# First projection of the last SwiGLU mixer: 19 of 22 tile pairs by seven half-size products

## The chip, the cores and the metric

The kernel runs on one core of a Trainium2 chip. The metric is the device time of one execution in microseconds. A core has a matrix engine (PE, whose weight loads are listed as PEld), a vector engine (DVE), an activation engine (ACT), a general engine (POOL), and a queue engine (SP) that issues most transfers. They run side by side, each through its own instructions in order, and wait for each other by semaphores. Matmuls write to PSUM, eight banks of 128 x 512 float32 numbers.

## The reference, cut to what matters

A decoder trunk over 512 tokens of width 1024: a Mamba layer, a dense SwiGLU mixer, an attention layer, and a second SwiGLU mixer, which ends the kernel. The change is in the second mixer's first projection.

```python
def swiglu(h, w_in, w_out):
    a, b = jnp.split(h @ w_in, 2, axis=-1)
    return (jax.nn.silu(a) * b) @ w_out
...
    h = adaln(x, norm_pre_ffn[i], sh_f, sc_f)
    x = x + g_f[:, None, :] * rmsnorm(swiglu(h, ffn_w_in[i], ffn_w_out[i]), norm_post_ffn[i])
```

Here h is 512 x 1024, w_in 1024 x 5632 (a and b are 2816 columns each, 22 tiles of 128), w_out 2816 x 1024, all float32.

## The kernel before, in words

Every float32 factor x is split into two fp32r parts (`split`, lines 112 and 113): hi, a rounded copy that ACT makes, and lo = x - hi, which DVE makes. A product is then three matmuls (`mm3`, lines 133 to 135): hi by hi, hi by lo, lo by hi. A matmul has 128 x 128 weights and up to 512 moving columns.

The activations h stand transposed: 8 tiles (k) of 128 features by 512 tokens, each a pair (hi, lo). Weights come from memory in units of 128 x 1024, which are 8 blocks of 128 x 128 (512 KB). `split_unit` loads a unit into a `raw` buffer (4 of them) through SP and splits it into a `w` buffer (3 pairs).

In the mixer (`ffn`, i = 1), `win` walks over the tile pairs f = 0 to 21; a pair is one tile of a and one of b, so two units. The first three pairs go through `linear_start`: the six units are split into held `b` tiles, and all six banks are filled for the first 256 tokens and then for the other 256, since the second half of h is finished later. Each of the other 19 pairs is two calls of `linear` into the two `acc` banks: 8 k by 3 matmuls of 512 columns each. Then ACT takes Silu of a (L425), DVE multiplies by b (L426) and the result is split into `mid` (L112, L113). After the last pair `project_out` makes the second projection (L276 to L278) with `mid` as its weights, first for output columns 0 to 511 into four `seg` banks (22 k by 4 by 3 matmuls), then for the other 512.

The second half of h comes from the attention layer's output: x is written (L346), its rows are scaled (`unit_rows`, with the small `rsqrt` steps L186 to L199 on DVE), turned by PE transposes (L240), scaled and shifted (L248, L250) and split.

The order of instructions on each engine is laid down when the program is built, by a planner: program order is the priority, an instruction is placed when its inputs and buffers are due by the planner's own estimates, and so an engine can be given later work ahead of earlier work that would wait. On the chip that order is fixed. Tiles of a pool with n buffers make the n+1st wait for the release of the first. The pools that matter are `rawp` (raw), `wp` (w), `t2` (8 small work tiles, named t), `b4` (33 tiles of 4 KB a partition, named b), and PSUM with 2 acc, 4 seg and 2 mi banks.

Of the kernel before, what the change touches and what calls it, by code (L numbers as in the profile page):

```python
# [9 lines left out]
F32 = mybir.dt.float32  # L10
F32R = mybir.dt.float32r
BF16 = mybir.dt.bfloat16
I32 = mybir.dt.int32
AF = mybir.ActivationFunctionType
OP = mybir.AluOpType
AX = mybir.AxisListType

P = 128
# [3 lines left out]
KD = D // P  # L22
KF = DFF // P
# [9 lines left out]
HALVES = [slice(0, S // 2), slice(S // 2, S)]  # L33
# [7 lines left out]
class Weights:  # L41


    def __init__(self, kern, dram, start=0):
        self.kern, self.dram = kern, dram
        self.unit, self.skip, self.left = start // 8, start % 8, 0
        self.queue = []
# [21 lines left out]
        return [(hi[:, i * P:(i + 1) * P], lo[:, i * P:(i + 1) * P]) for i in range(8)]  # L69


class Kernel:
    def __init__(self, ctx, tc, a):
        self.tc, self.nc, self.a = tc, tc.nc, a
        pool = lambda name, bufs=1, **kw: ctx.enter_context(tc.tile_pool(name=name, bufs=bufs, **kw))
        self.const = pool("const")
        self.rawp = pool("rawp", 4)
        self.wp = pool("wp", 3)
        self.t2 = pool("t2", 8)
        self.b4 = pool("b4", 33)  # L80
        self.small = pool("small", 2)
        self.psum = pool("psum", 3, space=bass.MemoryType.PSUM)
        self.dram = pool("dram", 1, space=bass.MemoryType.DRAM)
# [35 lines left out]
    def split_unit(self, dram, held=False):  # L119
        nc = self.nc  # L120
        raw = self.rawp.tile([P, 1024], F32, name="raw")
        nc.sync.dma_start(raw, dram)
        if held:
            hi, lo = self.big((P, 1024), F32R), self.big((P, 1024), F32R)
        else:
            w = self.wp.tile([P, 2, 1024], F32R, name="w")
            hi, lo = w[:, 0], w[:, 1]
        self.split(hi, lo, raw)
        return hi, lo

    def mm3(self, ps, wh, wl, xh, xl, start, stop):
        nc = self.nc
        nc.tensor.matmul(ps, wh, xh, start=start, stop=False)  # L133
        nc.tensor.matmul(ps, wh, xl, start=False, stop=False)  # L134
        nc.tensor.matmul(ps, wl, xh, start=False, stop=stop)  # L135

    def linear(self, weights, x, ps=None):

        ps = self.acc() if ps is None else ps
        for k, (xh, xl) in enumerate(x):  # L140
            wh, wl = weights.next()
            self.mm3(ps, wh, wl, xh, xl, k == 0, k == len(x) - 1)
        return ps

    def linear_start(self, weights, x, count, parts):

# [268 lines left out]
    def ffn(self, i, h, x_src, x_dst):  # L415
        nc = self.nc
        win = Weights(self, self.a[f"ffn_in{i}"])
        mods = [] if i else list(range(40, 112))
        start, each = MODS_FFN
        mid = []  # L420
        pss = self.linear_start(win, h, 6, HALVES)
        for f in range(KF):
            pa, pb = pss[2 * f:2 * f + 2] if f < 3 else (self.linear(win, h), self.linear(win, h))
            s = self.tmp()
            nc.scalar.activation(s, pa, AF.Silu)  # L425
            nc.vector.tensor_tensor(out=s, in0=s, in1=pb, op=OP.mult)  # L426
            m = self.big(dt=F32R)
            self.split(m[:, 0], m[:, 1], s)
            mid.append((m[:, 0], m[:, 1]))
            if f >= start:  # L430
                for j in mods[(f - start) * each:(f - start + 1) * each]:
                    self.mod(j, j in MODS_BEHIND)
        gain = self.scale_cols(("post_ffn", 8 * i), 48 * i + 40, 0.0)
        first = [self.seg() for _ in range(4)]
        if i:
            return self.project_out(self.a["ffn_out1"], mid, x_src, gain, x_dst, first)
        keep = [self.big() for _ in range(KD // 2)]
        keep = [keep[k // 2][:, k % 2] for k in range(KD)]
        h, after = self.before(("kv_norm", 0), 96, keep)
        self.project_out(self.a["ffn_out0"], mid, x_src, gain, x_dst, first, after)  # L440
        return h, keep


    def conv(self, ps, j):
# [628 lines left out]
CST_M, _ = _places([("tri", 128), ("mask_t", 128)])  # L1073
CST_A, _ = _places([("mask_q", 128), ("add_pe", 128), ("cmp_add", 128), ("cmp_ok", 128)])
# [25 lines left out]
def _blocks(w, order):  # L1100

    k, n = w.shape
    b = w.reshape(k // P, P, n // P, P).transpose(0, 2, 1, 3)
    i = np.array(order)
    b = b[i[:, 0], i[:, 1]]
    return np.ascontiguousarray(b.reshape(-1, 8, P, P).transpose(0, 2, 1, 3)).reshape(-1, P, 8 * P)


def _plain(w, tiles=None):
    k, n = w.shape[0] // P, w.shape[1] // P  # L1110
    return _blocks(w, [(i, j) for j in (range(n) if tiles is None else tiles) for i in range(k)])
# [14 lines left out]
def prepare(i):  # L1126
    g = {k: np.asarray(v) for k, v in i.items()}
# [19 lines left out]
                          + [(k, n) for n in tiles[6:] for k in range(KD)])  # L1147
    r["ssm_out"] = _halves(g["ssm_w_out"][0])
    for j in range(2):
        tiles = [t for f in range(KF) for t in (f, KF + f)]  # L1150
        r[f"ffn_in{j}"] = _plain(g["ffn_w_in"][j], tiles)
        r[f"ffn_out{j}"] = _halves(g["ffn_w_out"][j])
    w = g["w_kv"]
    k = _plain(w, [0, 1, 2, 3, 4, 5, 8, 9])
# [25 lines left out]
```

## Time and profile before

| | us |
|---|---|
| median of 3 runs (1556.65 to 1556.98) | 1556.92 |
| profiled execution, its own time | 1556.36 |
| its span from first to last instruction | 1554.3 |
| PE busy | 1485.1 |
| DVE busy | 997.8 |
| ACT busy | 710.3 |
| POOL busy | 83.2 |

Times on the timeline count from the first instruction. In a row of the timeline stand the start, the duration, the engine, the line, the operation, what it writes and reads, the shape and the count, and in brackets the idle time before it and what ended it. A matmul's duration contains the drain of the array, so the distance from one start to the next is its cost in a stream. Consecutive DVE operations overlap by some 0.08 us in the same way.

### The profile page before, as it was taken

The page shows a single profiled execution, that of the slowest core. Times are in us where ns is not written, and L with a number is a line of the kernel's source. Part 1 is how long each engine was busy: PE and PEld are TensorE (multiplying, and loading weights), DVE is VectorE, ACT ScalarE, POOL GpSimd, SP SyncE. Part 2 cuts the span into 40 slices and gives each one's busy share as a digit, 9 for nine tenths or more (in the row PEclk, how much of TensorE's full clock was granted, in tenths as well). Part 3 has the DMA queues.
Part 4 walks back from the last instruction along what each step waited for, and adds up shares of the span by engine and source line. Part 5 has one row for each costly group of instructions (what it writes and reads, how often), then busy time and mean ns, then how long its engine had stood idle before and what let it go on. Part 6 is the DMA issues. An engine that isn't in the chain of part 4 may idle for free.

```text
span 1554.3 us, 20592 instructions
## 1 busy us (share of the span) xinstructions
PE 1485.1 (96%) x7806; PEld 1204.2 (77%) x7806; DVE 997.8 (64%) x1798; ACT 710.3 (46%) x1216; POOL 83.2 (5%) x91
## 2 busy tenths in 40 slices
PE   6999899999999999999999999999999999999998
PEld 4767676767889787888889877777678888888886
DVE  7876776788594887862366778878857233333246
ACT  3574839384463223232366565555646222222233
POOL 0040303040000000000000100000000000000000
PEclk9999999999999999999999999999999999999999
DMA  8443253455672888863565452312244122232254
GB/s 297 160 137 101 63 166 92 149 176 204 233 249 70 304 297 288 287 241 102 182 205 204 113 170 62 82 42 69 55 163 149 41 95 98 99 103 95 95 203 149
DMA packets 71956, 236.62 MB, mean 152 GB/s; under 512 B 8465, under 2 KB 12049, under 8 KB 71858
## 3 DMA queue, kind: packets, MB, share of 16 engines
q1 hardware_dynamic: 71570, 235.07, 45.8%
q8 instruction: 61, 1.00, 0.3%
q10 hardware_dynamic: 288, 0.25, 0.1%
q14 instruction: 37, 0.30, 0.1%
HBM read 215.30 MB, written 8.45 MB: 144 GB/s over the span
## 4 chain that ended last, share of the span: by engine, by line
PE 66%; DVE 13%; DMA 10%; issue 5%; ACT 4%; POOL 1%; SPq 1%; DVEq 0%; ACTq 0%; POOLq 0%
PE acc L133 10%; PE acc L134 10%; PE acc L135 10%; PE seg L277 5%; PE seg L278 5%; PE seg L276 5%; DMA raw<-in_mod_dram 3%; PE acc L277 3%; PE acc L278 3%; PE acc L276 3%; DVE w L113 2%; DVE raw L160 2%; DMA raw<-in_ffn_in_dram 2%; PE mi L1030 2%; DMA b<-b 2%
## 5 line engine op out<-in xcount | busy, mean ns | idle before, releaser
L113 DVE TENSOR_TENSOR w<-raw,w 128x1024 fp32r<-128x1024 f32 x233 | 289.1, 1242 | 259.9 <-ACT w L112 259.3
L112 ACT ACTIVATE w<-raw 128x1024 fp32r<-128x1024 f32 x233 | 245.8, 1057 | 373.0 <-PE seg L278 121.2
L133 PE MATMUL acc<-b,w 128*128 128x512 f32 x976 | 388.8, 399 | 12.5 <-ACT w L112 4.9
L134 PE MATMUL acc<-b,w 128*128 128x512 f32 x976 | 385.1, 395 | 0.8 <-DVE b L113 0.8
L135 PE MATMUL acc<-b,w 128*128 128x512 f32 x976 | 385.1, 395 | 0.1
L133 PEld LDWEIGHTS acc<-b,w 128*128 128x128 f32 x976 | 184.6, 190 | 55.7 <-ACT w L112 6.1
L135 PEld LDWEIGHTS acc<-b,w 128*128 128x128 f32 x976 | 184.9, 189 | 40.6 <-issue 1.6
L134 PEld LDWEIGHTS acc<-b,w 128*128 128x128 f32 x976 | 185.3, 190 | 39.5 <-DVE b L113 1.9
L160 DVE SCALAR_TENSOR_TENSOR raw<-raw,b 128x1024 f32<-128x1024 f32 x112 | 137.5, 1235 | 26.9 <-DMA raw<-in_mod_dram 25.8
L276 PE MATMUL seg<-w,b 128*128 128x512 f32 x340 | 132.7, 391 | 0.0
L278 PE MATMUL seg<-w,b 128*128 128x512 f32 x340 | 132.6, 390 | 0.0
L277 PE MATMUL seg<-w,b 128*128 128x512 f32 x340 | 132.3, 389 | 0.0
L999 ACT ACTIVATE b<-seg,nm 128x512 f32<-128x512 f32 (+3 forms) x128 | 66.0, 525 | 51.8 <-DVE nm L994 49.3
L112 ACT ACTIVATE b<-t 128x512 fp32r<-128x512 f32 (+1 forms) x108 | 55.1, 529 | 49.2 <-DVE t L426 39.5
L278 PEld LDWEIGHTS seg<-w,b 128*128 128x128 f32 x340 | 63.8, 188 | 13.3
L277 PEld LDWEIGHTS seg<-w,b 128*128 128x128 f32 x340 | 63.8, 188 | 13.1
L276 PEld LDWEIGHTS seg<-w,b 128*128 128x128 f32 x340 | 63.9, 188 | 13.0
L426 DVE TENSOR_TENSOR t<-t,acc 128x512 f32<-128x512 f32 x40 | 27.4, 685 | 63.0 <-PE acc L135 63.0
L425 ACT ACTIVATE t<-acc 128x512 f32<-128x512 f32 x40 | 23.7, 593 | 94.5 <-PE acc L135 94.4
L276 PE MATMUL acc<-w,b 128*128 128x512 f32 x164 | 64.0, 392 | 1.6 <-ACT w L112 1.6
L277 PE MATMUL acc<-w,b 128*128 128x512 f32 x164 | 64.1, 391 | 1.3 <-DVE w L113 1.3
L113 DVE TENSOR_TENSOR b<-t,b 128x512 fp32r<-128x512 f32 (+1 forms) x108 | 59.1, 567 | 8.4 <-ACT b L112 8.2
(287 smaller groups left out, 2396.0 us busy)
## 6 DMA issues: line engine op xcount, KB each, us to landing
raw<-in_mod_dram SPq DMA_DIRECT2D x112, 512.0 KB, 4.6
raw<-in_ffn_in_dram SPq DMA_DIRECT2D x88, 512.0 KB, 4.4
raw<-in_ffn_out_dram SPq DMA_DIRECT2D x66, 512.0 KB, 3.7
raw<-in_ssm_in_dram SPq DMA_DIRECT2D x41, 512.0 KB, 4.3
raw<-in_ssm_out_dram SPq DMA_DIRECT2D x24, 512.0 KB, 4.4
b<-acsd SPq DMA_DIRECT2D x40, 256.0 KB, 5.8
b<-b SPq DMA_DIRECT2D x32, 256.0 KB, 4.7
raw<-in_kv_dram SPq DMA_DIRECT2D x12, 512.0 KB, 4.4
```

The lines of the kernel that those rows point to most:

```text
L112: nc.scalar.activation(hi, src, AF.Copy)
L113: nc.vector.tensor_tensor(out=lo, in0=src, in1=hi.bitcast(F32), op=OP.subtract)
L133: nc.tensor.matmul(ps, wh, xh, start=start, stop=False)
L134: nc.tensor.matmul(ps, wh, xl, start=False, stop=False)
L135: nc.tensor.matmul(ps, wl, xh, start=False, stop=stop)
L160: i = nc.vector.scalar_tensor_tensor(out=raw, in0=raw, scalar=1.0, in1=self.cs, op0=OP.mult, op1=OP.mult, accum_out=self.modc[:, n:n + 1])
L276: nc.tensor.matmul(ps, x[0][:, ts], wh, start=start, stop=False)
L277: nc.tensor.matmul(ps, x[0][:, ts], wl, start=False, stop=False)
L278: nc.tensor.matmul(ps, x[1][:, ts], wh, start=False, stop=stop)
L426: nc.vector.tensor_tensor(out=s, in0=s, in1=pb, op=OP.mult)
L999: nc.scalar.activation(p[i], bank[:, at:at + n], AF.Exp, bias=nm[:, i:i + 1], accum_out=d[:, i:i + 1])
L1030: nc.tensor.transpose(ps[:, i * n + a * P:i * n + (a + 1) * P], unit["p"][j * per + i][:, a * P:(a + 1) * P], self.ident)
```

## The change

For the 19 pairs f = 3 to 21 of the last mixer, the product of h (2 halves of tokens by 2 halves of k) with the pair's weights (2 halves of k by the two tiles a and b) is made as a 2 x 2 block product by seven products of half size instead of eight (the Winograd form of Strassen's method). With A for h and B for the weights, the left sums are s1 = a21 + a22, s2 = s1 - a11, s3 = a11 - a21, s4 = a12 - s2, and the right ones t1 = b12 - b11, t2 = b22 - t1, t3 = b22 - b12, t4 = b21 - t2.

- `factors` makes s1 to s4 once: DVE adds hi and lo of h back together (16 sums of 256 columns), POOL forms 8 sums of 512, and each is split.
- `seven` goes over the pairs. For each it loads two raw units, POOL forms t1 to t4 (512 columns each, in a new pool `st` of 5 tiles), and seven halves are split one by one (`split_half`, 512 columns). A product is 4 k by 3 matmuls of 256 columns. Three partial sums stay in PSUM and are read out between products by ACT copies and DVE adds into `pa` and `pb`; b1 takes five of the products one after another, and each copy of it stands between two. The products with b22 and t4 are made one pair late, between the first and the later products of the next pair, followed by Silu and two DVE multiplications (`done`).
- `mid` is kept unsplit (`Late`) and split where the second projection first uses it.
- A `w` buffer is now 4 KB, and there are 6. The blocks of w_in for the 19 pairs are reordered so that a unit holds 4 k of a and 4 k of b.

```diff
...
+class Late:
+    def __init__(self, kern):
+        self.kern, self.flat, self.made = kern, [], {}
+    def add(self, x):
+        self.flat.append(x)
+    def __len__(self):
+        return len(self.flat)
+    def __getitem__(self, k):
+        if k not in self.made:
+            m = self.kern.big(dt=F32R)
+            self.kern.split(m[:, 0], m[:, 1], self.flat[k])
+            self.made[k] = (m[:, 0], m[:, 1])
+        return self.made[k]
...
-        self.wp = pool("wp", 3)
+        self.wp = pool("wp", 6)
...
-            w = self.wp.tile([P, 2, 1024], F32R, name="w")
-            hi, lo = w[:, 0], w[:, 1]
+            hi, lo = (self.wp.tile([P, 1024], F32R, name="w") for _ in range(2))
...
+    def product(self, ps, x, w, start):
+        for k in range(4):
+            ks = slice(k * P, (k + 1) * P)
+            self.mm3(ps, w[:, 0, ks], w[:, 1, ks], x[k][0], x[k][1], start and k == 0, k == 3, more=True)
+    def factors(self, h):
+        nc = self.nc
+        part = lambda k0, sl: [(h[k][0][:, sl], h[k][1][:, sl]) for k in range(k0, k0 + 4)]
+        out = {"a11": part(0, HALVES[0]), "a12": part(4, HALVES[0]), "a22": part(4, HALVES[1]),
+               "s1": [], "s2": [], "s3": [], "s4": []}
+        for ks in (slice(0, 2), slice(2, 4)):
+            u = {}
+            for name, k0, sl in (("11", 0, HALVES[0]), ("12", 4, HALVES[0]), ("21", 0, HALVES[1]), ("22", 4, HALVES[1])):
+                u[name] = self.tmp((P, 2, 256))
+                for k in range(2):
+                    hi, lo = h[k0 + ks.start + k]
+                    nc.vector.tensor_tensor(out=u[name][:, k], in0=hi[:, sl].bitcast(F32), in1=lo[:, sl].bitcast(F32),
+                                            op=OP.add)
+            s1, s2, s3, s4 = (self.tmp((P, 2, 256)) for _ in range(4))
+            nc.gpsimd.tensor_tensor(out=s1, in0=u["21"], in1=u["22"], op=OP.add)
+            nc.gpsimd.tensor_tensor(out=s2, in0=s1, in1=u["11"], op=OP.subtract)
+            nc.gpsimd.tensor_tensor(out=s3, in0=u["11"], in1=u["21"], op=OP.subtract)
+            nc.gpsimd.tensor_tensor(out=s4, in0=u["12"], in1=s2, op=OP.subtract)
+            for name, s in (("s2", s2), ("s3", s3), ("s1", s1), ("s4", s4)):
+                t = self.big((P, 2, 2, 256), F32R)
+                self.split(t[:, 0], t[:, 1], s)
+                out[name] += [(t[:, 0, k], t[:, 1, k]) for k in range(2)]
+        return out
+    def seven(self, dram, units, x, done):
+        nc = self.nc
+        def rights(i):
+            xr, yr = (self.rawp.tile([P, 1024], F32, name="raw") for _ in range(2))
+            nc.sync.dma_start(xr, dram[i])
+            nc.sync.dma_start(yr, dram[i + 1])
+            b11, b12, b21, b22 = xr[:, 0:512], xr[:, 512:1024], yr[:, 0:512], yr[:, 512:1024]
+            t1, t2, t3, t4 = (self.st.tile([P, 512], F32, name="st") for _ in range(4))
+            nc.gpsimd.tensor_tensor(out=t1, in0=b12, in1=b11, op=OP.subtract)
+            nc.gpsimd.tensor_tensor(out=t2, in0=b22, in1=t1, op=OP.subtract)
+            nc.gpsimd.tensor_tensor(out=t3, in0=b22, in1=b12, op=OP.subtract)
+            nc.gpsimd.tensor_tensor(out=t4, in0=b21, in1=t2, op=OP.subtract)
+            out = {}
+            for name, src in (("b11", b11), ("b21", b21), ("t2", t2), ("t3", t3), ("t1", t1), ("b22", b22), ("t4", t4)):
+                out[name] = (lambda src=src: self.split_half(src))
+            return out
+        late = None
+        for i in list(units) + [None]:
+            if i is not None:
+                w = rights(i)
+                one, two = self.acc(), self.seg()
+                pa, pb = self.tmp(), self.tmp((P, 256))
+                b1, b2, b3 = one[:, 0:256], two[:, 0:256], two[:, 256:512]
+                self.product(b1, x["a11"], w["b11"](), True)
+                nc.scalar.activation(pa[:, 0:256], b1, AF.Copy)
+                self.product(b3, x["a12"], w["b21"](), True)
+                nc.vector.tensor_tensor(out=pa[:, 0:256], in0=pa[:, 0:256], in1=b3, op=OP.add)
+            if late is not None:
+                j, lw, l1, l2, la, lb = late
+                self.product(l1, x["s4"], lw["b22"](), False)
+                self.product(l2, x["a22"], lw["t4"](), False)
+                nc.vector.tensor_tensor(out=la[:, 256:512], in0=la[:, 256:512], in1=l2, op=OP.add)
+                done(j, la, lb, l1)
+                late = None
+            if i is not None:
+                self.product(b1, x["s2"], w["t2"](), False)
+                nc.scalar.activation(pa[:, 256:512], b1, AF.Copy)
+                self.product(b2, x["s3"], w["t3"](), True)
+                self.product(b1, x["s1"], w["t1"](), False)
+                nc.scalar.activation(pb, b1, AF.Copy)
+                nc.vector.tensor_tensor(out=pb, in0=pb, in1=b2, op=OP.add)
+                late = (i, w, b1, b2, pa, pb)
+    def split_half(self, src):
+        w = self.wp.tile([P, 2, 512], F32R, name="w")
+        self.split(w[:, 0], w[:, 1], src)
+        return w
...
+        if i:
+            return self.ffn_seven(win, h, pss, x_src, x_dst)
...
-        if i:
-            return self.project_out(self.a["ffn_out1"], mid, x_src, gain, x_dst, first)
...
+    def ffn_seven(self, win, h, pss, x_src, x_dst):
+        nc = self.nc
+        mid = Late(self)
+        flat = []
+        def tile(f):
+            if f % 2 == 0:
+                flat.append(self.big())
+            return flat[f // 2][:, f % 2]
+        for f in range(3):
+            pa, pb = pss[2 * f:2 * f + 2]
+            s = self.tmp()
+            nc.scalar.activation(s, pa, AF.Silu)
+            m = tile(f)
+            nc.vector.tensor_tensor(out=m, in0=s, in1=pb, op=OP.mult)
+            mid.add(m)
+        x = self.factors(h)
+        def done(i, a, b, b1):
+            nc.scalar.activation(a, a, AF.Silu)
+            m = tile(i // 2)
+            nc.vector.tensor_tensor(out=m[:, 0:256], in0=a[:, 0:256], in1=b1, op=OP.mult)
+            nc.vector.tensor_tensor(out=m[:, 256:512], in0=a[:, 256:512], in1=b, op=OP.mult)
+            mid.add(m)
+        with ExitStack() as es:
+            self.st = es.enter_context(self.tc.tile_pool(name="seven", bufs=5))
+            self.seven(self.a["ffn_in1"], range(6, 2 * KF, 2), x, done)
+        gain = self.scale_cols(("post_ffn", 8), 48 + 40, 0.0)
+        return self.project_out(self.a["ffn_out1"], mid, x_src, gain, x_dst, [self.seg() for _ in range(4)])
...
-        tiles = [t for f in range(KF) for t in (f, KF + f)]
-        r[f"ffn_in{j}"] = _plain(g["ffn_w_in"][j], tiles)
+        n = 3 if j else KF
+        order = [(k, t) for f in range(n) for t in (f, KF + f) for k in range(KD)]
+        order += [(k, t) for f in range(n, KF) for h in range(2) for t in (f, KF + f) for k in range(4 * h, 4 * h + 4)]
+        r[f"ffn_in{j}"] = _blocks(g["ffn_w_in"][j], order)
...
```

## Rows read from the trace of the kernel before

**Rows 1.** The page's busy times: us, share of the span, instructions.

```profile
PE 1485.1 (96%) x7806; PEld 1204.2 (77%) x7806; DVE 997.8 (64%) x1798; ACT 710.3 (46%) x1216; POOL 83.2 (5%) x91
```

**Rows 2.** Busy time by stage: PE, PEld, DVE, ACT, POOL, granted clock, DMA.

```profile
1224.00:1426.00 202.00, 202.00 (x894) 167.22 (x893) 68.56 (x73) 57.84 (x74) 0.00 (x0) 1.00 0.29 96
1426.00:1486.00 60.00, 60.00 (x270) 49.80 (x269) 15.34 (x14) 14.45 (x18) 0.00 (x0) 1.00 0.29 96
```

**Rows 3.** Timeline of ACT and PE between 1246 and 1301 us.

```profile
1246.49 0.60 ACT L425 ACTIVATE t<-acc 128x512 f32<-128x512 f32 x1 [3.81 <-PE acc L135]
...
1257.37 0.60 ACT L425 ACTIVATE t<-acc 128x512 f32<-128x512 f32 x1 [3.81 <-PE acc L135]
...
1300.47 0.39 PE L135 MATMUL acc<-b,w 128*128 128x512 f32 x1
...
1300.89 0.60 ACT L425 ACTIVATE t<-acc 128x512 f32<-128x512 f32 x1 [3.81 <-PE acc L135]
```

**Rows 4.** Timeline of PE between 1206 and 1220 us.

```profile
1206.47 0.28 PE L133 MATMUL acc<-b,b 128*128 128x256 f32 x1
...
1210.79 0.28 PE L133 MATMUL seg<-b,b 128*128 128x256 f32 x1
...
1219.07 0.40 PE L133 MATMUL acc<-b,w 128*128 128x512 f32 x1
```

**Rows 5.** Groups of DVE and ACT after 1140 us: busy us, mean ns, idle.

```profile
L113 DVE TENSOR_TENSOR w<-raw,w 128x1024 fp32r<-128x1024 f32 x71 | 86.9, 1225 | 147.9 <-ACT w L112 147.9
...
L112 ACT ACTIVATE b<-t 128x512 fp32r<-128x512 f32 x22 | 13.6, 618 | 8.3 <-DVE t L426 8.3
L425 ACT ACTIVATE t<-acc 128x512 f32<-128x512 f32 x20 | 12.0, 598 | 72.7 <-PE acc L135 72.7
...
L112 ACT ACTIVATE b<-t 128x256 fp32r<-128x256 f32 x16 | 5.9, 408 | 0.1
```

**Rows 6.** Timeline of DVE: starts of consecutive operations.

```profile
322.02 0.68 DVE L641 TENSOR_TENSOR b<-mi,tdt 128x512 f32<-128x512 f32 x1
322.62 0.68 DVE L638 TENSOR_TENSOR b<-mi,dt 128x512 f32<-128x512 f32 x1
...
1202.86 0.75 DVE L113 TENSOR_TENSOR b<-t,b 128x256 fp32r<-128x256 f32 x2
```

**Rows 7.** Timeline of POOL.

```profile
90.50 0.72 POOL L600 TENSOR_TENSOR b<-b,b 128x256 f32<-128x256 f32 x1
...
327.37 1.71 POOL L598 TENSOR_TENSOR b<-b,b 128x256 f32<-128x256 f32 x1
...
963.09 1.28 POOL L700 TENSOR_TENSOR t<-t,b 128x512 f32<-128x512 f32 x1 [21.56 <-DVE t L699]
```

**Rows 8.** Timeline of DVE beside POOL's sums, 326 to 335 us.

```profile
326.74 1.75 DVE L113 TENSOR_TENSOR w<-raw,w 128x1024 fp32r<-128x1024 f32 x1
...
331.09 0.15 DVE L164 TENSOR_TENSOR modc<-modc,vec 128x1 f32<-128x1 f32 x1
...
334.35 0.70 DVE L164 TENSOR_TENSOR modc<-modc,vec 128x1 f32<-128x1 f32 x1
```

**Rows 9.** Timeline of ACT, DVE and PE before the held-weight start ends.

```profile
1189.30 1.06 ACT L112 ACTIVATE w<-raw 128x1024 fp32r<-128x1024 f32 x1 [0.57 <-DMA raw<-in_ffn_in_dram]
1190.63 1.06 ACT L112 ACTIVATE w<-raw 128x1024 fp32r<-128x1024 f32 x1 [0.27 <-DMA raw<-in_ffn_in_dram]
...
1190.10 2.48 DVE L346 SCALAR_TENSOR_TENSOR b<-b,y,b 128x1024 f32<-128x1024 f32 x2
...
1197.91 0.75 DVE L231 TENSOR_SCALAR b<-b,y 128x1024 f32<-128x1024 f32 x1
...
1203.99 1.08 DVE L113 TENSOR_TENSOR b<-t,b 128x256 fp32r<-128x256 f32 x3
...
1198.81 0.41 PE L240 MATMUL mi<-ident,b 128*128 128x128 f32 x2 [1.47 <-DVE b L231]
```

More of the change, by code (lines that the diff above doesn't have):

```diff
@@ L125, in split_unit, with mm3 @@
         else:
-            w = self.wp.tile([P, 2, 1024], F32R, name="w")
-            hi, lo = w[:, 0], w[:, 1]
+            hi, lo = (self.wp.tile([P, 1024], F32R, name="w") for _ in range(2))
         self.split(hi, lo, raw)
         return hi, lo
-    def mm3(self, ps, wh, wl, xh, xl, start, stop):
+    def mm3(self, ps, wh, wl, xh, xl, start, stop, more=False):
         nc = self.nc
-        nc.tensor.matmul(ps, wh, xh, start=start, stop=False)
-        nc.tensor.matmul(ps, wh, xl, start=False, stop=False)
-        nc.tensor.matmul(ps, wl, xh, start=False, stop=stop)
+        nc.tensor.matmul(ps, wh, xh, start=start, stop=False, skip_group_check=more)
+        nc.tensor.matmul(ps, wh, xl, start=False, stop=False, skip_group_check=more)
+        nc.tensor.matmul(ps, wl, xh, start=False, stop=stop, skip_group_check=more)
     def linear(self, weights, x, ps=None):
```

## The prediction

> **What bounds the kernel now.** I read the page's busy shares first: PE is busy 96% of the span and POOL hardly at all [rows 1]. Then busy time by stage. The change sits in the stage from 1224 to 1426 us, the plain part of the last mixer's first projection: PE has no idle there, the granted clock is 1.00 (its 2.4 GHz level), DVE is busy 68.56 and ACT 57.84 of 202 us, POOL 0 [rows 2]. Then the timeline inside it: the Silu of one tile pair starts 10.88 us after that of the pair before [rows 3]. A pair is 2 tiles x 8 k x 3 matmuls = 48 matmuls of 512 columns, so one costs 10.88 / 48 = 0.2267 us. Nothing else ends later than PE here; what counts is PE's time and whatever new wait stops it. The 19 pairs that change take 19 x 10.88 = 206.7 us, from 1219.07 on [rows 4].
>
> **PE's part.** Seven products of 4 k x 3 matmuls are 84 matmuls of 256 columns a pair. Such matmuls, each with its own weight load, are in the trace: the held-weight start of this same mixer runs them 36 in a row from 1206.47 to 1210.79, 0.120 us each [rows 4], through changes of bank and without a gap. So a pair costs 84 x 0.120 = 10.08 us. Columns fall by an eighth (84 x 256 against 48 x 512), PE's time only by 0.80 us (7.4%), because each matmul costs 0.0133 us beyond its share of columns. 19 pairs give 15.2 us. That the weight load (one per 0.120 us) might bind is excluded by the same rows.
>
> **What the other engines must do in one pair.** ACT: seven splits of 512 (0.62), three copies of 256 out of PSUM (nearest row 0.41), one Silu (0.60) [rows 5]: 6.2 us of 10.08, enough room. DVE: seven subtracts of 512, one started every 0.60 us (322.02 to 322.62), and five operations of 256 at 0.375 (two in 0.75) [rows 6]: 4.2 + 1.9 = 6.1 us, against 1.2 x 2 + 1.4 before. POOL: four sums of 512; the nearest row with DVE reading PSUM only beside it is 1.28 us [rows 7], so 5.1 us. Each engine alone fits below PE's 10.08.
>
> **Together they may not.** Where POOL's sums meet DVE operations with two SBUF inputs, both grow: a POOL sum of 256 takes 0.72 beside DVE work on PSUM and 1.71 beside DVE's subtract of 1024 [rows 7], and that subtract takes 1.75 [rows 8] where its mean is 1.225 [rows 5]; even a DVE operation on one column takes 0.70 instead of 0.15 [rows 8]. So a POOL sum of 256 costs DVE 0.525, one of 512 about 1.05. Eight of DVE's twelve operations a pair have two SBUF inputs (seven subtracts, one product); four read PSUM. Bounds of DVE's need: no meeting, 6.1; all four sums in its way, 6.1 + 4 x 1.05 = 10.3; the PSUM ones running under POOL's, some 1.5 less, 8.8; strict turns (DVE's eight 4.6, POOL's 5.1, and the PSUM four after them 1.5), 11.2.
>
> The Trainium skill (SBUF — State Buffer, section "Who interferes with whom") says that a DVE instruction with two SBUF inputs and a GpSimd instruction that reads SBUF exclude each other for a whole instruction, while one with an SBUF input at most does not. The rows just given agree in kind; the exchange is a little cheaper than strict turns (1.75 where 1.225 + 0.72 would be 1.95). By strict turns with nothing beneath them a pair would be 11.2 and the change a loss; by the rows it is 8.8 to 10.3, around PE's 10.08.
>
> PE does not follow DVE at once. Six halves of weights are split ahead (six buffers of which a product uses one), some 5 x 1.44 = 7.2 us, and raw loads, 4 buffers, are due a pair ahead. The tight place is ACT: between the product with t2 and that with t1, both into b1, the copy of b1 has one product, 1.44 us. Alone it is ready 0.19 (a Silu starts 1300.89, the last matmul's slot ends 1300.47 + 0.23 [rows 3]) + 0.41 = 0.60 after t2's end. But the Silu in `done` stands ahead of it on ACT, and waits for a DVE add into la after t4; PE, its next products done, then waits for ACT. With one POOL sum and one subtract ahead of that add: 0.19 + 1.28 + 0.60 + 0.375 + 0.60 + 0.41 = 3.45 us after t4's end, where PE wants b1 at 2.88: a stall of 0.57. I take 0.20 us a pair over 10.08 (such a stall in a pair of three, DVE otherwise just within PE's time): 3.8 us. The bounds are 0 and 11.2 - 10.08 = 1.1 us a pair.
>
> **The start.** Two costs. First, while the second half of h is made, raw units land at 1189.30 and 1190.63, and in the new order POOL can begin the first unit's four sums then; the chain that makes h runs on DVE from 1190.10 (x written) over the rsqrt steps to 1197.91, PE having stood idle 1.47 us for it at 1198.81 [rows 9]. Four sums at up to 1.05 are 0 to 4.2 us on the path; DVE has free places there, so I take 2.0. Second, the left factors: from the last h at 1205.07 (1203.99 + 1.08 [rows 9]) to the first use of s2, 1219.07 + 2 x 1.44 = 1221.95, are 16.9 us. Before it DVE has 16 sums of 256 (6.0), five subtracts (3.0), three Silu products (1.8), and six POOL sums in its way (up to 6.3): at most 17.1. I take 0.5 of a range 0 to 2. Start: 2.5 us.
>
> **Costed at nothing.** The 22 splits of mid move into the second projection: 22 x 0.62 on ACT and 22 x 0.60 on DVE, beside 14.45 and 15.34 busy of 60 us there [rows 2], POOL idle; without that cover they would be 13.6 us. The first k needs its split early, but the tiles of the first pairs lie ready for long. The bytes and DMA issues are unchanged, two 512 KB loads a pair at 96 GB/s [rows 2]. `wp` with 6 halves of the old size is the same memory in finer pieces. The last pair's two late products replace no wait.
>
> **Sum.** 15.2 - 3.8 - 2.5 = 8.9 us. From the profiled execution's own time of 1556.36 (span 1554.3 and 2.06 around it) that gives 1547.5; the median of the three runs is 0.56 above that execution: 1548.0 us.
>
> **Rivals.** 0.2%, 3.1 us, is what a measurement of this kernel tells from no change.
> - *Nothing is late* (0.21): pairs at 10.08 and a free start: 1556.9 - 15.2 = 1541.7. For it: every engine alone has room, and buffers cover 7 us. Against it: the grown durations in [rows 7, 8], and a chain that PE already waited for [rows 9].
> - *DVE becomes the bound* (0.16): DVE and POOL so often in each other's way that a pair takes 10.4 to 11.2, say 10.75: 19 x 0.13 = 2.5 won, 2.5 lost at the start: 1556.9, no change. For it: needs of up to 10.3 against 10.08. Against: when DVE is idle POOL runs alone, and the PSUM operations don't meet it.
> - *Slower: PE waits for the copy of b1 in nearly every pair* (0.13). Place: the t1 product, behind Silu and the add into la. Price: 0.57 with one POOL sum ahead, with two sums and two subtracts 1.28 + 0.60 more, 2.45; the mean of both, 1.5, gives 11.58 a pair: 19 x 0.70 + 2.5 = 15.8 more: 1572.7. It decides from (15.2 - 2.5) / 19 = 0.67 us a pair on, which a single sum ahead does not reach. For it: DVE and ACT both work their queues in order. Against: POOL is busy only half of the pair, and the add comes soon after an earlier subtract is through.
>
> That the change doesn't do what it says has no chance worth a number: the 256-column rate is in the trace.
>
> **How the numbers follow.** The forecast has 0.50, with 1544 to 1553 of its own (0 to 0.4 us a pair, 1 to 4 at the start). Faster by over 0.2% (below 1553.8) are it, but for 0.01, and the first rival: 0.70. Within 0.2%: the second rival and that 0.01: 0.17. Slower: 0.13. The range 1541 to 1558 holds the forecast, the first rival but for its lower edge, and two thirds of the second: 8 in 10. The slower rival is left out.
>
> **What would show each step.** Right: in the stage from 1219 us, Silus of the new loop some 10.3 us apart, matmuls of 256 at 0.120 within a product, gaps of PE ahead of the t1 product and released by ACT; DVE's subtracts of 512 between 0.69 and 1.9; POOL's sums between 1.3 and 2; PE's wait at the transposes of the second half of h longer by 1 to 3 us; the second projection still at 0.227 a matmul. Wrong: a rate inside products other than 0.120; PE waiting on weights w (DVE as the bound) rather than on b1; POOL never longer than 1.3; or a stage elsewhere in the kernel moved by the finer weight buffers.

## The result, and the profile after

The changed kernel takes 1563.87 us (median of 4 runs, 1561.83 to 1564.48) where the kernel before takes 1556.79: ratio 1.0051, 95% interval 1.0033 to 1.0070. It is slower by 7 us. I had forecast 1548.0, faster by 9. Its profiled execution has a span of 1562.0 us, 7.7 more than before.

The page of the changed kernel: busy us, share of the span, instructions; then busy tenths in 40 slices and the granted clock in tenths.

```profile
PE 1472.4 (94%) x8490; PEld 1229.8 (79%) x8490; DVE 1120.2 (72%) x1993; ACT 773.6 (50%) x1376; POOL 218.4 (14%) x175
...
PE   6989898999999999999999989999997799999998
...
PEclk9999999999999999999999999999998899999999
```

PE is busy 12.7 us less than in [rows 1]; the end comes later all the same, so PE idles some 20 us more. The slices say where: only two in the middle (about 1171 to 1249 us) show 7 and a clock of 8. Windows of the changed kernel (PE, PEld, DVE, ACT, POOL busy, granted clock, DMA share, GB/s):

```profile
1200.00:1210.00 10.00, 2.67 (x13) 2.70 (x14) 7.28 (x16) 2.02 (x3) 4.46 (x3) 0.61 0.15 53
...
1240.00:1250.00 10.00, 3.99 (x18) 4.00 (x19) 5.91 (x7) 4.10 (x8) 7.71 (x6) 0.50 0.15 52
...
1260.00:1420.00 160.00, 160.00 (x1336) 160.00 (x1335) 140.30 (x191) 91.31 (x175) 107.00 (x64) 1.00 0.31 103
1435.00:1495.00 60.00, 60.00 (x268) 49.73 (x267) 27.50 (x36) 23.12 (x37) 0.00 (x0) 1.00 0.33 114
```

From 1260 to 1495 us PE never stops. The loss is two holes ahead of that, which the timeline of PE shows (in brackets the idle time before, and what ended it):

```profile
1180.20 0.38 PE L152 MATMUL acc<-b,b 128*128 128x256 f32 x1 [1.04 <-ACT b L132]
...
1207.33 0.66 PE L344 MATMUL mi<-ident,b 128*128 128x128 f32 x2 [8.05 <-DVE b L335]
...
1229.73 0.28 PE L152 MATMUL acc<-b,w 128*128 128x256 f32 x1
...
1238.50 0.38 PE L154 MATMUL seg<-b,w 128*128 128x256 f32 x1 [2.75 <-DVE w L133]
...
1246.01 0.58 PE L152 MATMUL acc<-b,w 128*128 128x256 f32 x1 [6.05 <-ACT t L225]
...
1247.03 0.41 PE L153 MATMUL acc<-b,w 128*128 128x256 f32 x1
1247.24 0.41 PE L154 MATMUL acc<-b,w 128*128 128x256 f32 x1
```

The first row, the start of the last mixer, I call the marker; before, it stands at 1179.62, as the row of that kernel's timeline shows:

```profile
1179.62 0.38 PE L133 MATMUL acc<-b,b 128*128 128x256 f32 x1 [1.04 <-ACT b L112]
```

Its time differs from one profile to another (1178.48 to 1189.59 over all runs here), by work ahead of the mixer, where the change alters only the weight buffers; so stages are compared from it. Before: 19.19 us to the transposes of the second half of h (1198.81, [rows 9]), 39.45 to the first of the 19 pairs (1219.07, [rows 4]), 374.68 to the end. After: 27.13, 49.53 (1229.73) and 381.80. So the first hole costs 49.53 - 39.45 = 10.08 us: 7.94 until the transposes, and 2.14 from there on, where PE first runs at half clock (0.50 granted from 1207.3 to 1212). From 1229.73 to the end of the pairs at 1435.27 are 205.54 us; taking off 19 x 10.08 = 191.52 and 1.87 of other matmuls that run in between, 12.15 are lost: waits of 2.75, 6.05, 0.17 and 0.47, half clock from 1246 to 1250 (0.213 a matmul, not 0.120: some 1.8), and shorter gaps. Together, -15.2 + 10.08 + 12.15 = 7.03; from marker to end 7.12 are measured.

**First hole.** POOL of the changed kernel, and DVE beside it:

```profile
1189.34 1.80 POOL L208 TENSOR_TENSOR st<-raw 128x512 f32<-128x512 f32 x1 [93.98 <-DMA raw<-in_ffn_in_dram]
...
1199.79 1.59 POOL L209 TENSOR_TENSOR st<-raw,st 128x512 f32<-128x512 f32 x1 [0.68 <-POOL st L208]
1201.34 1.26 POOL L210 TENSOR_TENSOR st<-raw 128x512 f32<-128x512 f32 x1
1203.36 1.86 POOL L211 TENSOR_TENSOR st<-raw,st 128x512 f32<-128x512 f32 x1 [0.76 <-DVE w L133]
```
```profile
1191.69 4.55 DVE L450 SCALAR_TENSOR_TENSOR b<-b,y,b 128x1024 f32<-128x1024 f32 x2
...
1200.18 1.22 DVE L290 TENSOR_SCALAR v<-sx 128x2 f32<-128x2 f32 x1
1201.43 1.19 DVE L292 TENSOR_SCALAR y<-v 128x2 int32<-128x2 int32 x1
...
1204.00 1.24 DVE L303 SCALAR_TENSOR_TENSOR y<-t,y 128x2 f32<-128x2 f32 x1
...
1206.43 0.75 DVE L335 TENSOR_SCALAR b<-b,y 128x1024 f32<-128x1024 f32 x1
...
1214.48 1.09 DVE L133 TENSOR_TENSOR b<-t,b 128x256 fp32r<-128x256 f32 x3
...
1224.24 0.69 DVE L562 TENSOR_TENSOR b<-t,seg 128x512 f32<-128x512 f32 x1 [5.07 <-PE seg L154]
1224.85 2.77 DVE L182 TENSOR_TENSOR t<-b 128x256 f32<-128x256 f32 x8
...
1235.42 2.42 DVE L182 TENSOR_TENSOR t<-b 128x256 f32<-128x256 f32 x7
1237.77 1.28 DVE L133 TENSOR_TENSOR w<-raw,w 128x512 fp32r<-128x512 f32 x2
```

Between 1189.34 and 1205.22 POOL forms eight sums, those of two pairs. The write of x takes 4.55 us instead of 2.48 [rows 9], and rsqrt steps on two columns 1.2, where before they took 0.16:

```profile
1195.97 0.16 DVE L188 TENSOR_SCALAR y<-v 128x2 int32<-128x2 int32 x1
```

None of these operations uses a sum of POOL, and each of the three long steps shown ends 0.02 us after a sum of POOL does (1201.40 after 1201.38, 1202.62 after 1202.60, 1205.24 after 1205.22).

**Second hole.** h is complete at 1215.57 (1214.48 + 1.09), but the sums of hi and lo (L182) start at 1224.85: in DVE's order they stand behind the product of the second plain pair (L562), which waits for PE. ACT of the changed kernel:

```profile
1245.05 0.63 ACT L132 ACTIVATE b<-t 128x512 fp32r<-128x512 f32 x1 [0.52 <-POOL t L188]
1245.59 0.37 ACT L225 ACTIVATE t<-acc 128x256 f32<-128x256 f32 x1
...
1260.32 0.38 ACT L240 ACTIVATE t<-acc 128x256 f32<-128x256 f32 x1 [0.73 <-PE acc L154]
...
1270.40 0.38 ACT L240 ACTIVATE t<-acc 128x256 f32<-128x256 f32 x1 [0.72 <-PE acc L154]
```

The copy of b1 (L225) stands behind the last split of a left factor, which waits for POOL; b1's last matmul had started at 1231.05. That is the wait of 6.05 us. The wait of 2.75 us ahead of it is for a weight: DVE subtracts it at 1237.77, behind the sums of the second set of factors (1235.42). In the steady loop (L240, one a pair) the distance is 10.08 us.

### The profile page after: what moved, and what is told of

The parts are those of the page before. It is cut to its first block, busy times and chain, and to the rows that moved or that the text cites. A ratio compares the mean times of both kernels' runs of the same rounds, so it can differ in the third digit from the quotient of the medians.

```text
span 1562.0 us, 22600 instructions
## 1 busy us (share of the span) xinstructions
PE 1472.4 (94%) x8490; PEld 1229.8 (79%) x8490; DVE 1120.2 (72%) x1993; ACT 773.6 (50%) x1376; POOL 218.4 (14%) x175
## 4 chain that ended last, share of the span: by engine, by line
PE 68%; DVE 13%; DMA 8%; issue 5%; ACT 3%; POOL 1%; SPq 0%; DVEq 0%; ACTq 0%; POOLq 0%
PE acc L152 9%; PE acc L153 9%; PE acc L154 9%; PE seg L381 5%; PE seg L382 5%; PE seg L380 4%; PE acc L381 3%; PE acc L382 3%; PE acc L380 3%; DVE w L133 3%; DMA raw<-in_mod_dram 2%; PE seg L154 2%; PE seg L153 2%; PE seg L152 2%; DMA b<-b 2%
## 5 line engine op out<-in xcount | busy, mean ns | idle before, releaser
L133 DVE TENSOR_TENSOR w<-raw,w 128x1024 fp32r<-128x1024 f32 (+1 forms) x252 | 308.2, 1229 | 181.8 <-ACT w L132 174.9
L132 ACT ACTIVATE w<-raw 128x1024 fp32r<-128x1024 f32 (+1 forms) x252 | 241.8, 961 | 386.2 <-PE seg L381 122.4
L152 PE MATMUL acc<-b,w 128*128 128x512 f32 (+1 forms) x976 | 357.5, 367 | 20.8 <-ACT w L132 7.0
L154 PE MATMUL acc<-b,w 128*128 128x512 f32 (+1 forms) x976 | 352.8, 361 | 0.5 <-DVE w L133 0.5
L153 PE MATMUL acc<-b,w 128*128 128x512 f32 (+1 forms) x976 | 351.9, 361 | 0.6 <-DVE b L133 0.6
L836 POOL TENSOR_TENSOR t<-t,b 128x512 f32<-128x512 f32 x12 | 18.4, 1530 | 728.2 <-DVE t L835 728.2
L154 PE MATMUL seg<-b,w 128*128 128x256 f32 (+1 forms) x276 | 84.3, 305 | 4.1 <-DVE w L133 4.1
L153 PE MATMUL seg<-b,w 128*128 128x256 f32 (+1 forms) x276 | 84.1, 305 | 0.0
L152 PE MATMUL seg<-b,w 128*128 128x256 f32 (+1 forms) x276 | 82.8, 305 | 0.2 <-ACT w L132 0.2
L133 DVE TENSOR_TENSOR w<-st,w 128x512 fp32r<-128x512 f32 x76 | 63.4, 838 | 16.9 <-ACT w L132 14.0
L132 ACT ACTIVATE b<-t 128x256 fp32r<-128x256 f32 (+1 forms) x94 | 46.4, 517 | 51.1 <-DVE t L532 29.9
```

Source lines behind the costliest of these rows:

```text
L132: nc.scalar.activation(hi, src, AF.Copy)
L133: nc.vector.tensor_tensor(out=lo, in0=src, in1=hi.bitcast(F32), op=OP.subtract)
L152: nc.tensor.matmul(ps, wh, xh, start=start, stop=False, skip_group_check=more)
L153: nc.tensor.matmul(ps, wh, xl, start=False, stop=False, skip_group_check=more)
L154: nc.tensor.matmul(ps, wl, xh, start=False, stop=stop, skip_group_check=more)
L836: nc.gpsimd.tensor_tensor(out=sw, in0=sw, in1=self.sin, op=OP.mult)
```

## The experiments

All are the changed kernel with the edit named. "To the end" is from the marker to the end of the span; "lost" is that, less before's 374.68, plus 0.80 us for each pair that goes by seven products (15.2 for 19, 14.4 for 18). The kernel before, run again beside them, has medians of 1555.6 to 1555.9.

| kernel | median us | ratio to before (95%) | to the end | lost | PE waits at transposes; around the first new pair |
|---|---|---|---|---|---|
| changed | 1563.87 | 1.0051 (1.0033 to 1.0070) | 381.80 | 22.3 | 8.05; 2.75, 6.05 |
| e4_blank | 1556.03 (1 run) | | 372.35 | 12.9 | 1.46; 2.75, 5.01 |
| e5_hold_second | 1555.99 (1 run) | | 375.72 | 16.2 | 3.52; 2.75, 5.10 |
| e1_hold | 1557.51 | 1.0011 (0.9994 to 1.0029) | 373.43 | 14.0 | 1.18; 2.52, 2.14, 5.01 |
| f1_no_factors | 1554.32 | 0.9984 (0.9964 to 1.0004) | 369.57 | 10.1 | 7.74; none |
| f2_hold_no_factors | 1542.08 | 0.9899 (0.9858 to 0.9940) | 359.44 | 0.0 | none; none |
| e2_early | 1560.74 | 1.0039 (1.0019 to 1.0059) | 377.41 | 17.9 | 7.73; 6.24 |
| e6_direct | 1557.93 | 1.0013 (1.0003 to 1.0023) | 375.58 | 16.1 | 9.48; 3.91 |
| e8 | 1555.35 | 1.0002 (0.9988 to 1.0017) | 373.12 | 13.6 | 1.03; 8.51, 1.73 |
| f3_four | 1561.94 | 1.0030 (1.0011 to 1.0050) | 378.28 | 18.0 | 4.58; 3.04, 4.28 |
| f4_hold_four | 1553.94 | 0.9985 (0.9965 to 1.0005) | 371.29 | 11.0 | none; 3.18, 2.30 |
| e10_four_hold | 1547.87 | 0.9947 (0.9927 to 0.9968) | 363.81 | 3.5 | none; 1.73, 1.31 |
| e11_four_hold2 | 1544.90 | 0.9929 (0.9912 to 0.9946) | 362.87 | 2.6 | none; 0.51, 1.05 |

### The first hole: POOL's early sums, or the new order of DVE's queue?

**e4_blank**: POOL's eight early sums are left out; writes of zeros, which read nothing, stand in their place.

```diff
+            if i in (6, 8):
+                for t in (t1, t2, t3, t4):
+                    for _ in range(3):
+                        nc.gpsimd.memset(t, 0.0)
+            else:
```

> The eight right sums that POOL makes before the last half of h (two units) become three memsets of 512 columns each: POOL is busy for as long but reads nothing; t1 to t4 of these two units hold zeros, so their 2 pairs are not the reference's. DVE's order is that of the changed kernel. Theory A (POOL's reads hold DVE operations with two SBUF inputs): the write of x takes 2.5 us instead of 4.55, the rsqrt steps 3.2 instead of 6.3, PE waits about 1.5 us at the transposes instead of 8.05, the seven-product stage starts near 1220 us instead of 1229.7, and the time falls by about 10 us to 1554. Rival B (the subtracts of the new halves stand ahead of the chain in DVE's queue): order unchanged, so the wait stays at 7 to 8 us and the time at 1562 to 1564.

DVE of this kernel, in the same order of work, then POOL:

```profile
1192.53 2.48 DVE L455 SCALAR_TENSOR_TENSOR b<-b,y,b 128x1024 f32<-128x1024 f32 x2
...
1196.75 0.17 DVE L295 TENSOR_SCALAR v<-sx 128x2 f32<-128x2 f32 x1
1196.96 0.46 DVE L297 TENSOR_SCALAR y<-v 128x2 int32<-128x2 int32 x1
...
1198.75 0.15 DVE L308 SCALAR_TENSOR_TENSOR y<-t,y 128x2 f32<-128x2 f32 x1
```
```profile
1131.19 7.58 POOL L211 MEMSET st<- 128x512 f32 x15 [33.17 <-DVE d L1148]
1196.27 5.05 POOL L211 MEMSET st<- 128x512 f32 x9 [57.49 <-DVE w L133]
```

The write of x is back at 2.48. POOL isn't busy for as long as was expected: fifteen of the writes run before 1139 us, and the write of x meets none. The small steps do run beside the other nine and take 0.15 to 0.17, but for one of 0.46. From the marker to the transposes it is 19.05 us, to the first new pair 39.38: the first hole is gone, the second is there. So it is POOL's sums that hold DVE; the rival, the order of the queue, falls. This run alone doesn't tell a hold by the sums' reads from splits that wait for their results, since most of the zeros lay ready early; the long steps of the changed kernel do, as they use no result of POOL.

**e5_hold_second** and **e1_hold**: sums of unit pair 8 alone, or of 6 and 8, wait for the last part of h, by a one-column copy on POOL ahead of them.

```diff
+            if i in (6, 8):       # e5: (8,)
+                for t in (t1, t2, t3, t4):
+                    nc.gpsimd.tensor_copy(out=t[:, 0:1], in_=x["a22"][3][1][:, 255:256].bitcast(F32))
```

> Only the second unit's four right sums are held back until h is complete (a one-column copy out of h into each sum's tile ahead of it). Theory A, each sum costing DVE about 1.05 us: the chain's lateness halves from 8.5 to 4 us, PE's wait at the transposes is 4 to 5 us, the time near 1558. Rival B (queue order): four of the subtracts that stood in the chain go too, some 2.4 us, wait 5.5 to 6 us, 1561. If only the first sums matter the wait stays at 8.

> The right sums of the first two units are held back until h is complete. Theory A: PE's wait at the transposes returns to about 1.5 us, no half clock follows, the seven-product stage starts near 1220 us and the time falls by 9 to 10 us, to about 1554: about equal to before, because the factor stall (some 12 us) stays. Rival: the held sums come due too late for the first products and the gain is given back there, 1560 or more.

To the transposes it is 27.13 us with eight sums in the way and 19.05 in e4_blank, where DVE has the same queue without them: 1.0 us a sum. With four it is 22.59, which is 3.4 more than before (19.19) and 5.3 more than with none in e1_hold (17.32; the splits of the held sums are out of the way too), so 0.85 to 1.3 each. The wait of 3.52 in e5_hold_second is under the expected 4 to 5. In e1_hold the first new pair starts 39.10 us after the marker, and the second hole remains whole. It even grows: from that pair to the end are 334.33 us, 2.06 more than in the changed kernel, with a new wait of 2.52 for a split weight. So its rival was right in part, and the median is 3.5 us above the expected 1554.

### The second hole: making the left factors

**f1_no_factors**: the factors are left out; **f2_hold_no_factors**: that and e1_hold's copies.

```diff
-        for ks in (slice(0, 2), slice(2, 4)):
...
+        for name in ("s1", "s2", "s3", "s4"):
+            out[name] = out["a11"]
```

> Leaves out the left factors (16 sums, 8 sums on POOL, their splits): a11 stands in all products in place of s1 to s4; nothing else differs from the changed kernel. Theory (making the left factors costs 12.15 us by itself, beside and not instead of the late h): no wait of PE in the first new pair, while the wait of some 8 us at the transposes stays; 1563.9 - 12.15 = 1551.7, and from the marker to the end some 369.7 (381.8 in the changed kernel). Rival (the first new pair is late for its own right factors, the left ones only come on top): waits of 4 us or more remain there, 1556 or more.

> As the run before, without the left factors, and POOL's sums of the first two unit pairs wait for the last part of h. Theory (late h and late left factors together are all that stood against the gain of the 19 pairs): 1556.8 - 15.2 = 1541.6, from the marker to the end 374.7 - 15.2 = 359.5 (up to 361). Rival (something else in the changed kernel costs as well, the mid splits in the second projection, the finer weight buffers, the waits on b1): 1545 or more, 363 or more from the marker.

From the marker to the end 369.57 and 359.44 us, where 369.7 and 359.5 were expected. Windows of f2_hold_no_factors, the first new pairs and the loop:

```profile
1220.00:1230.00 10.00, 10.00 (x85) 10.00 (x85) 3.49 (x6) 3.67 (x7) 1.51 (x2) 1.00 0.30 102
...
1250.00:1410.00 160.00, 160.00 (x1335) 160.00 (x1335) 135.88 (x189) 91.26 (x174) 102.77 (x60) 1.00 0.32 105
```

With both holes closed PE has no wait after the marker but for 0.76 at the next matmul (there before too), and the whole 15.2 us appear. From the marker on nothing else in the change costs anything that shows. f1's median is 2.6 us above the expected 1551.7; its profile has the marker 2.7 later than the changed kernel's, and what follows the marker is as expected.

**e2_early**: the call that makes the factors moves ahead of the three Silus.

```diff
+        x = self.factors(h)
         for f in range(3):
...
-        x = self.factors(h)
```

> The call that makes the left factors stands ahead of the three Silus in program order instead of behind them; nothing else changes. Theory C (work buffers of a pool are handed out in program order, so the factors' first sums had to wait for the buffers of the Silus of the held-weight start): DVE's sums of h start within 1 us after the last h, the PE waits in the first pair (6.05 and 2.75 us) shrink below 3 us together, and the time falls by 9 to 12 us to about 1553. Rival D (DVE and POOL simply need that long for 16 sums, 8 sums and 8 splits beside each other): the sums start earlier but PE's waits stay above 6 us, time above 1558. In both the wait at the transposes stays at 8 us.

A miss in its cost: the sums of hi and lo come right after h, but ACT takes the first Silu only at 1239.07, behind factor splits that wait for POOL, and PE waits 6.24 us for its bank. The waits within the first new pair are gone; what is left moved along ACT's queue.

**e6_direct** lets only the sums move: the Silus no longer hold one of the eight work tiles. **e8** is that, and sums of unit pair 6 held until h, those of 8 until the last left factor.

```diff
-            s = self.tmp()
-            nc.scalar.activation(s, pa, AF.Silu)
             m = tile(f)
-            nc.vector.tensor_tensor(out=m, in0=s, in1=pb, op=OP.mult)
+            nc.scalar.activation(m, pa, AF.Silu)
+            nc.vector.tensor_tensor(out=m, in0=m, in1=pb, op=OP.mult)
```

> The Silus of the first three pairs are written straight into their tile of the second projection, so the sums of hi and lo need not wait for the work tile that a Silu holds, and ACT keeps its order. Theory (in the factor phase it is the place in the queues that costs: the sums of hi and lo stood behind the product of the second pair on DVE): they start within 2 us of the last part of h (9.3 us after it in the changed kernel), the waits of 2.75 and 6.05 us in the first new pair shrink to 3 us or less together, the clock there stays at 2.4 GHz, and the time falls by about 9 us below the changed kernel, to about 1554; the wait of some 8 us at the transposes stays. Rival (the sums and splits of the factors are in themselves too much work for the time, wherever they stand): the waits in the first new pair stay at 6 us or more together, and the time stays above 1558.

> Silus written straight as in the run before, and POOL's sums held back: those of the first unit pair until the last part of h is made, those of the second until the last left factor is split. Theory (the two start costs, 10.1 and 12.15 us, are all that turned the gain into a loss): wait at the transposes 1 to 2 us, from the marker to the first new product 39 to 40 us, waits in the first new pair 0 to 4 us, pairs at 10.08: 1556.8 - 15.2 + (0 to 4) = 1541.6 to 1545.6. Rival (the loss lies elsewhere too, or the held sums are now late themselves, the first pair's t2 waiting for POOL): 1549 or more, with PE waits of 6 us or more in the first new pair.

e6_direct wins 6.2 of the 9 us; one wait of 3.91 is left in place of two that make 8.80, above the 3 us of its theory, and half clock behind it (0.50 from 1235 to 1239). e8 misses by 10 us, and its rival came true: against e1_hold it wins 0.3. Its ACT, DVE, POOL and PE:

```profile
1219.04 2.18 ACT L132 ACTIVATE b<-t 128x512 fp32r<-128x512 f32 x4
...
1231.82 0.63 ACT L132 ACTIVATE b<-t 128x512 fp32r<-128x512 f32 x1 [0.53 <-POOL t L188]
1232.35 0.37 ACT L229 ACTIVATE t<-acc 128x256 f32<-128x256 f32 x1
```
```profile
1221.81 1.28 DVE L133 TENSOR_TENSOR w<-st,w 128x512 fp32r<-128x512 f32 x2
...
1224.21 1.88 DVE L133 TENSOR_TENSOR b<-t,b 128x512 fp32r<-128x512 f32 x3
```
```profile
1225.03 2.19 POOL L185 TENSOR_TENSOR t<-t,t 128x512 f32<-128x512 f32 x1 [5.11 <-DVE b L133]
```
```profile
1232.77 0.58 PE L152 MATMUL acc<-b,w 128*128 128x256 f32 x1 [8.51 <-ACT t L229]
```

The factors are made in two sets of eight work tiles each, and there are eight. ACT splits the first set from 1219.04, right behind the third Silu, but DVE only from 1224.21, behind splits of the first pair's weights (1221.81), which came late with the held sums. Only then has POOL tiles for the second set (1225.03), and the copy of b1 stands on ACT behind its last split (1232.35). So PE reaches this wait 9.66 us earlier after the marker than in e6_direct (41.98 against 51.64) and leaves it only 5.06 earlier (50.49 against 55.55).

### Cover: one more plain pair

**f3_four**: a fourth pair by eight products, on the changed kernel; **f4_hold_four**: on e1_hold.

```diff
-        for f in range(3):
-            pa, pb = pss[2 * f:2 * f + 2]
+        for f in range(4):
+            pa, pb = pss[2 * f:2 * f + 2] if f < 3 else (self.linear(win, h), self.linear(win, h))
...
-            self.seven(self.a["ffn_in1"], range(6, 2 * KF, 2), x, done)
+            self.seven(self.a["ffn_in1"], range(8, 2 * KF, 2), x, done)
```

> The changed kernel with one edit: the fourth pair also goes by eight products, seven products from the fifth on; nothing is held back. Theory (the left factors were late by about one plain pair): its 10.88 us cover them, and 12.15 falls to 3 or less for a gain smaller by 0.80: 1563.9 - 9 to 11.4 = 1552.5 to 1555, marker to end 370.5 to 373; the wait of some 8 us at the transposes stays. Rival (the sums of hi and lo stand behind the next Silu product whatever the cover, and are late again): waits of 5 us or more in the first new pair, 1557 or more.

> The plain fourth pair, and POOL's sums of the first two unit pairs of the new loop wait for the last part of h; the Silus still go through the work tile. Theory (holding and cover are enough, where the Silu is written matters little once the plain pair is there): marker to end 361 to 364, time 1543 to 1549. Rival (with the Silus in work tiles the sums of hi and lo come a pair later and eat the cover): 366 or more from the marker, waits of 4 us or more in the first new pair, 1550 or more.

Both went as their rivals said in time; the waits reach the rivals' figures only taken together. f4_hold_four wins 2.1 us (371.29 against 373.43) by 10.88 us of cover, f3_four 3.5 (378.28 against 381.80). But f3_four's gain is not the cover's. Its POOL forms five sums early instead of eight, as its row of the last one and PE's of the first product after the held-weight start show:

```profile
1207.07 1.26 POOL L208 TENSOR_TENSOR st<-raw 128x512 f32<-128x512 f32 x1
```
```profile
1234.24 0.40 PE L152 MATMUL acc<-b,w 128*128 128x512 f32 x1
```

So that product starts 46.32 us after the marker, not 49.53, and from there to the end it is 331.96 us, not 332.27: of the 3.5, 3.2 come from a smaller first hole. DVE of f3_four shows why the cover brings so little:

```profile
1234.51 0.69 DVE L562 TENSOR_TENSOR b<-t,seg 128x512 f32<-128x512 f32 x1 [5.07 <-PE seg L154]
1235.12 2.77 DVE L182 TENSOR_TENSOR t<-b 128x256 f32<-128x256 f32 x8
...
1245.98 0.67 DVE L562 TENSOR_TENSOR b<-t,acc 128x512 f32<-128x512 f32 x1
...
1248.89 2.42 DVE L182 TENSOR_TENSOR t<-b 128x256 f32<-128x256 f32 x7
```

The first set's sums now stand behind the third product, not the second, and most of the second set's behind the fourth. Against the start of the first new pair (1245.15; 1229.73 in the changed kernel) they come 5.1 and 2.0 us earlier, not 10.88: the work that makes the factors has queued behind its own cover.

**e10_four_hold**: cover, e1_hold's copies and the direct Silus; **e11_four_hold2**: the same, but the second unit pair's sums wait for the last left factor, as in e8.

> As the run before, but the fourth pair also goes by eight products, so that a further 10.88 us of PE work stand between h and the first use of a left factor; seven products over 18 pairs; the sums of the first two unit pairs wait for the last part of h. Theory (the left factors were late by less than one plain pair): no wait of PE over 1 us from the transposes to the end of the first new pair, clock 2.4 GHz throughout; gain 18 x 0.80 = 14.4: 1556.8 - 14.4 = 1542.4, up to 1544 with small waits. Rival (POOL with all held sums and the factors' sums at once makes the factors later by as much as the cover gives): waits of 4 us or more in the first new pair, 1547 or more.

> As the run before, with the sums of the second unit pair held until the last left factor is split, so that POOL has less ahead of the factors' sums. Theory: the same as there, 1542.4 to 1544, since the plain pair covers the factors either way; the left factors are split some 5 us earlier. Rival (what POOL has ahead of the factors decides): 3 us or more below the run before.

They lose 3.5 and 2.6 us and beat the kernel before by 0.5% and 0.7%. Both miss the 1542.4 to 1544 that was expected, e10_four_hold by 3.9 us with waits of 1.73 and 1.31, e11_four_hold2 by 0.9. PE of e11_four_hold2:

```profile
1233.26 0.39 PE L152 MATMUL acc<-b,w 128*128 128x256 f32 x1 [0.51 <-ACT b L564]
```

Net of the 0.80 us that one pair less by seven products gives up, cover is worth 2.1 us with the Silus in work tiles (e1_hold to f4_hold_four) and 10.3 with them direct and the sums held (e8 to e11_four_hold2). The two medians of e10 and e11 differ by 3.0 us, from the marker on only by 0.9, and their intervals overlap: which of the two holds is better stays open.

## Why the prediction was wrong

*The rate and the gain: right.* 10.08 us a pair was measured, 1336 matmuls in 160 us (0.120 each), and f2_hold_no_factors shows all of the 15.2 us.

*0.20 us a pair for engines in each other's way: it was nothing.* They do meet. Groups of the changed kernel between 1260 and 1420 us (busy us, mean ns, idle before):

```profile
L133 DVE TENSOR_TENSOR w<-raw,w 128x512 fp32r<-128x512 f32 x48 | 61.1, 1298 | 0.1
...
L208 POOL TENSOR_TENSOR st<-raw 128x512 f32<-128x512 f32 x16 | 28.0, 1753 | 52.1 <-DVE w L133 52.1
...
L240 ACT ACTIVATE t<-acc 128x256 f32<-128x256 f32 x16 | 6.1, 384 | 11.6 <-PE acc L154 11.6
```

A subtract of a raw half takes 1.30 us where 0.60 was its price alone, a sum 1.75 where 1.28 was; but DVE is busy 140.30 of 160 us, 8.8 a pair, which is the figure of the case "the PSUM ones running under POOL's". The copies of b1 wait for PE alone. So the bound stayed on PE, and the rival with DVE as the bound falls.

*The start: this step failed, 2.5 us where 22.2 were lost, and it turned the sign.* It has two parts.

"Four sums at up to 1.05 are 0 to 4.2 us on the path; DVE has free places there, so I take 2.0." The price was right (1.0 us a sum, the changed kernel against e4_blank), the count and the free places were not: the second unit pair had landed as well, the buffers let POOL go on, and eight sums met a DVE that was busy 6.79 of 7 us from 1200 to 1207. Measured: 7.94. And a wait of PE has a second price that the sum left out: 2.14 us at half clock.

The left factors, "0.5 of a range 0 to 2": I counted the work (17.1 us against 16.9 of room), and took it that the work begins when h is there. It begins where it stands in the queues. The planner had put it behind a product of DVE that waits for PE, in two sets through eight work tiles, and on ACT the copy that PE needs stands behind all its splits: 12.15 us. f1_no_factors shows that this is the whole price of the factors. e6_direct wins back 6.2 us by place alone, and e11_four_hold2, with the same work, loses 2.6 in all: place and cover decide most of it.

The slower rival ended on the right side by the wrong way: its stall, PE waiting for a copy of b1 behind other work on ACT, occurs (6.05 us), but once, at the start, and not in the loop.

*Costed at nothing: right.* In the second projection DVE and ACT are busy 27.50 and 23.12 of 60 us with mid's splits, PE 60.00. The finer weight buffers move nothing that the marker shows: 1180.20 against 1179.62. But it lies between 1178.48 and 1189.59 over the runs, so a cost of a few us ahead of it isn't excluded.

The Trainium skill (SBUF — State Buffer, section "Who interferes with whom") says that a GpSimd instruction that reads SBUF excludes a DVE instruction with two SBUF inputs, and one that only writes does not. The rows agree: the step with two tensor inputs that takes 1.24 us beside a sum (L303 of the changed kernel) takes 0.15 beside the writes of e4_blank (L308). The page counts a tensor_scalar, with its single tensor input, among those that can take the shared port as well, an exception that the prediction left out; the two of the rsqrt chain did meet the sums (1.22 and 1.19 us on two columns), and beside the writes they took 0.17 and 0.46.

Not tried: moving the copy of b1 ahead of the splits on ACT by itself, or giving the factors 16 work tiles.

## What to carry to other kernels

A faster inner loop is priced from its own rows, but its start is a stage of its own: for each new instruction there, read in the queue what stands ahead of it and what that waits for, and count every unit whose buffers allow it to run early, not only the first. Look first at small operations in a serial chain: here another engine's sums made 1.2 us out of 0.16. Covering a late input with more work helps only if the work that makes the input doesn't queue behind the cover.

## What the runs showed of the hardware

Sums of 512 columns on POOL stretched DVE operations on two columns from 0.16 to about 1.2 us, each ending 0.02 us after a sum. Beside writes of the same size (e4_blank) they took 0.15 to 0.17, but for one of 0.46. After PE's idle times of 8.05 and 6.05 us the granted clock was 0.50 (1.2 GHz), and matmuls of 256 columns came 0.213 us apart instead of 0.120, for some 4 us after the second. After the wait of 2.75 it was 1.00 (1238.50 to 1239.70). The clock also stood near 0.5 from 1.9 to 5 us after the marker in nine of the fourteen profiles (0.50 to 0.55), and at 1.00 in the other five, though all have the same waits of 1.04 and 0.76 us there; why stays open. A first half made at half clock leaves less to wait for at the transposes, 8.05 us in the changed kernel against 9.48 in e6_direct, which reaches them at the same distance from the marker (27.13 and 27.06).
